# A hybrid layer on one core: the last pair's factors made one half later, the mixer called one step earlier, the first gates fetched later

## The chip, the cores and the metric

The kernel runs on one core of one Trainium2 chip. The time is device microseconds of one execution; before the change three runs gave 2416.04, 2421.66 and 2422.43 us, the median being 2421.66 us. One more execution was profiled, and every row below is from it.

## The reference

One layer (`DEPTH = 1`) on 512 tokens of 2048 features, all in float32:

```python
proj = rms_norm(x, g_mix) @ w_in                    # q, k, v, u, v_sgu, gate_a, gate_b
y_a = stick_breaking_attention(q, k, v) @ w_oa      # 8 heads of 128, output 1024 wide
s   = gelu(u) * (w_s @ layer_norm(gelu(v_sgu)) + b) # 8 groups, 128 x 128 mixing per 128 tokens
y_b = s @ w_ob
x = x + (sigmoid(gate_a) * y_a + sigmoid(gate_b) * y_b) @ w_out
x = x + square(relu(rms_norm(x, g_ff) @ w_ff1)) @ w_ff2    # hidden width 8192
```

## The kernel before, in words

**Arithmetic.** A float32 product is made from two parts of each operand, `hi` (a copy rounded to fp32r, made by ScalarE) and `lo` (the rest, a subtraction on VectorE). The function `mm3` issues three matmuls for each product: hi by hi, hi by lo and lo by hi; they stand at L72, L73 and L74. A weight piece is loaded into `w_raw` by SyncE's DMA queue, cast to `w_hi` by ScalarE and subtracted to `w_lo` by VectorE (L99 and L101 in `weight`, L113 and L114 in `split_to`). The pool of weight pieces has six buffers, three pairs of hi and lo.

**Order of the work.** Each engine runs its instructions strictly in the order that a planner at build time has chosen. The planner replays the program on its own costs and takes, for each engine, the earliest traced instruction that it thinks ready, so a later one can be taken ahead when it thinks the engine free and a buffer is there. The text of the kernel gives the tracing order. Beside the main loops there is a queue of tasks called `behind`: after each weight piece (or, in the last product, after each of seven sub-products) the loop calls `step()`, which takes one entry off that queue. `at_steps(steps)` puts a table of tasks, numbered by step, into the queue. `let(f)` traces a tiny GpSimd instruction (L814) that reads the newest `w_lo`, and orders the DMA issues in `f` behind it on GpSimd's queue.

**The product stage** (about 795 to 987 us). `by_column` first makes `ya` = attention output by `w_oa` in four column blocks j of 512, four weight pieces each, so 16 steps numbered 0 to 15; then `yb` = gated mixer output by `w_ob`, steps 16 to 31. Block j of `ya` ends with `evac_a`: four VectorE multiplications by the gate (`merged_a`, L836), which also free the accumulators in PSUM; the pool has five, and a block uses four. The attention output comes back from device memory as 16 tiles `oT` (two for each of 8 heads) through GpSimd's DMA queue, line L508 in `fetched`; 12 of them go into the pool `long`, whose buffers come free as the last input projection ends. On the same queue are fetched the gates (`gates(which, j)`, four tiles of 256 KB for one block) and the mixer's inputs (`fetch_mix(half)`, eleven tiles: `wsp`, `bs`, `vn` and `u`).

The mixer is called by half (four groups each). `split_mix` normalises `vn` (L788) and splits it. `mixed(g)` does for one group: matmuls (L801, L803), four VectorE instructions (L806, L808), a GpSimd multiplication (L810) and the split into `sT` (ScalarE's cast L113, VectorE's subtraction L114). `step()` for the last piece of a block is traced ahead of that block's `evac_a`.

**The last product** (`w_ff2`, about 1798 us to the end). Eight chunks f of 1024 hidden features; each has two halves g of the output columns, and each half seven sub-products with the names y11, y21, m7, m6, y22, m4, m5: 14 steps for one chunk. `strassen_tokens` works on two groups i of weights; `Sums.parts` makes the sums of weights that the names need (L186, L190, L192, L194 on VectorE) and splits them. `evac_y` adds the sub-products into `total` (L1041, L1044). The factors of the hidden activations were stored in device memory, and `fetch` brings them back on GpSimd's queue (L1001). For the last two pairs of hidden features, 30 and 31, the seven factors are made while the last product already runs, by `keeping` (L251 in `factor`, L113 and L114 in `halves`, the store at L967 on SyncE's queue): pair 31, the last, in chunk 0 and pair 30 in chunk 1. They are read only in chunk 7.

Of the kernel before, what the change touches and what calls it, by code (L numbers as in the profile page):

```python
# [35 lines left out]
def tile_hybrid_layer(ctx: ExitStack, tc: tile.TileContext, x, g_mix, w_in, g_q, g_k, ln_g, ln_b,  # L36
# [17 lines left out]
    def slot(name, dt=F32, pool=slots):  # L54
        return pool.tile([P, 512], dt, name=name, tag="slot")
# [4 lines left out]
    def aux(name):  # L60
        return ps_aux.tile([P, 512], F32, name=name, tag="aux")

    def tiny(n, name):
        return small.tile([P, n], F32, name=name, tag=f"tiny{n}")

    def f32(ap):
        return ap.bitcast(F32)
# [8 lines left out]
    state = {"load": None, "raw": raws}  # L76
    behind = collections.deque()
# [27 lines left out]
    def split(src, name, scale=None, pool=slots):  # L105

        hi, lo = slot(name + "_hi", F32R, pool), slot(name + "_lo", F32R, pool)
        split_to(hi, lo, src, scale)
        return hi, lo
# [396 lines left out]
    def fetched(src, name, dt=F32, pool=slots):  # L506
        t = slot(name, dt, pool)
        nc.gpsimd.dma_start(out=f32(t) if dt is F32R else t, in_=src)  # L508
        return t
# [171 lines left out]
    def at_steps(steps):  # L681
        behind.extend([lambda fs=steps.get(i, []): [f() for f in fs] for i in range(max(steps) + 1)])

    VC = 2 * SBW
    for half in range(2):
# [4 lines left out]
        if half:  # L690
            steps = collections.defaultdict(list)
# [63 lines left out]
    for i, item in enumerate(order):  # L755
# [6 lines left out]
        else:  # L762
            c0, n, func = item
# [7 lines left out]
    def gates(which, j):  # L771
        n = SGW // P + which * (D // P) + j * 4
        return [fetched(held_g[n + c], "gate") for c in range(4)]
# [4 lines left out]
    def fetch_mix(half):  # L778
        wsT.extend(fetched(held_s[half * 2 + i], "wsp", F32R) for i in range(2))
        bs[half] = fetched(held_s[4 + half], "bs")  # L780
        for tb in range(NTB):
            vn[tb, half] = fetched(held_v[half, tb], "vn")
        u.extend(fetched(held_g[half * 4 + g], "u") for g in range(4))

    def split_mix(half, blocks):
        for tb in blocks:
            t = vn[tb, half]
            nc.vector.tensor_scalar(out=t, in0=t, scalar1=mv[:, tb, 0:1], scalar2=rv[:, tb:tb + 1],  # L788
                                    op0=ALU.subtract, op1=ALU.mult)
            vn[tb, half] = split(t, "vn")  # L790

    def mixed(g):
        half, c = g // 4, (g % 4) * P
        both = wsT[g // 2][:, (g % 2) * 2 * P:(g % 2 + 1) * 2 * P]
        t = slot("smix")
        for pair in range(2):

            o = aux("mix").rearrange("p (b h i) -> p b h i", b=2, h=2)
            for b in range(2):
                vh, vl = (p[:, c:c + P] for p in vn[pair * 2 + b, half])  # L800
                nc.tensor.matmul(o[:, b].rearrange("p h i -> p (h i)"), lhsT=vh, rhs=both, start=True,  # L801
                                 stop=False)
                nc.tensor.matmul(o[:, b, 1], lhsT=vl, rhs=both[:, :P], start=False, stop=True)  # L803
            t3 = t[:, pair * 2 * P:(pair + 1) * 2 * P].rearrange("p (b i) -> p b i", b=2)
            gain = gT2[:, 32 + g:33 + g]
            nc.vector.scalar_tensor_tensor(out=t3, in0=o[:, :, 1, :], scalar=gain, in1=bs[half][:, c:c + P]  # L806
                                           .unsqueeze(1).to_broadcast([P, 2, P]), op0=ALU.mult, op1=ALU.add)
            nc.vector.scalar_tensor_tensor(out=t3, in0=o[:, :, 0, :], scalar=gain, in1=t3, op0=ALU.mult,  # L808
                                           op1=ALU.add)
        nc.gpsimd.tensor_tensor(out=t, in0=t, in1=u[g], op=ALU.mult)  # L810
        sT.append(split(t, "sT"))

    def let(f):
        gate = nc.gpsimd.tensor_tensor(out=tiny(4, "gate"), in0=f32(state["piece"])[:, 0, :4], in1=mhalf,  # L814
                                       op=ALU.mult)
        with tc.issue_after(gate.ins):
            f()

    with tc.issue_after(state["sum"].ins):
        ahead = collections.deque([gates(0, 0)])  # L820
    steps = collections.defaultdict(list)
    for half in range(2):
        steps[1 + 5 * half].append(lambda half=half: let(lambda: fetch_mix(half)))
        for i in range(2):
            steps[4 + i + 5 * half].append(lambda half=half, i=i: split_mix(half, (2 * i, 2 * i + 1)))
    for g in range(GROUPS):
        steps[7 + g + g // 4].append(lambda g=g: mixed(g))
    for i, wj in enumerate([(0, 1), (0, 2), (0, 3), (1, 0), (1, 1), (1, 2), (1, 3)]):
        steps[4 * i].append(lambda wj=wj: let(lambda: ahead.append(gates(*wj))))
    at_steps(steps)  # L830

    merged_a = []
# [121 lines left out]
    def keeping(p, act):  # L954

        ys = {}

        def keep(name):
            if name == "y11":
                for a in act:  # L960
                    nc.scalar.activation(out=a, in_=a, func=AF.Square)
            if name in ("y11", "y21", "y22"):
                h = act[name[1] == "2"]
                ys[name, 0] = halves(h[:, :HS] if name[2] == "1" else h[:, HS:])
            else:
                factor(ys, act, 0, name)
            nc.sync.dma_start(out=store[p // GROUP][HELD.index(name), p % GROUP], in_=f32(ys[name, 0]))  # L967

        return [lambda name=name: keep(name) for name in ("y11", "y21", "y22", "m7", "m6", "m4", "m5")]
# [43 lines left out]
    kept_last = []  # L1013
# [15 lines left out]
    for f in range(chunks):  # L1029
        ahead = {}  # L1030
        if kept_last:
            for task in keeping(*kept_last.pop()):
                behind.extend([task, lambda: None])
        for g in range(2):
            def evac_y(name, t, o):
                for half, c, op in takes[name]:
                    key = 2 * half + t, 2 * g + c
                    part = share[op][:, 2 * half + t:2 * half + t + 1]
                    if key not in total:
                        total[key] = slot("total")  # L1040
                        nc.scalar.activation(out=total[key], in_=o, func=AF.Copy, scale=part)  # L1041
                    else:
                        a = total[key]
                        nc.vector.scalar_tensor_tensor(out=a, in0=o, scalar=part, in1=a, op0=ALU.mult,  # L1044
                                                       op1=ALU.add)
                if f == chunks - 1:
                    for half, c in done[g].get(name, []):
                        tb, j = 2 * half + t, 2 * g + c
                        nc.sync.dma_start(out=out[tb * P:(tb + 1) * P, j * W:(j + 1) * W], in_=total[tb, j])

            def between(name):


                i = NAMES.index(name)
                if f == 0:
                    half, c, _ = takes[name][0]
                    gate = nc.gpsimd.tensor_tensor(out=tiny(4, "gate"), in0=total[2 * half + 1, 2 * g + c][:, :4],
                                                   in1=mhalf, op=ALU.mult)
                    with tc.issue_after(gate.ins):
                        if g == 0 and i + 4 < len(NAMES):  # L1060
                            lhs[NAMES[i + 4]] = fetch(0, NAMES[i + 4])
                        if g == 1:
                            ahead[name] = fetch(1, name)
                    return
                if (f, g) in ((2, 1), (3, 0)):
                    for n in (i, len(NAMES)) if i == len(NAMES) - 1 else (i,):
                        tb, j = n % NTB, 2 * (1 - g) + n // NTB
                        nc.gpsimd.dma_start(out=total[tb, j], in_=kept[tb, j], accum_op=ALU.add)
                i += g * 5
                if f < chunks - 1 and i < (5 if g == 0 else 7):  # L1070
                    ahead[NAMES[i]] = fetch(f + 1, NAMES[i])

            strassen_tokens(w_ff2[0], f * GROUP * 2 * P, g * 2 * W, lhs, evac_y, between,
                            loaded=f > 0, after=None if f or g else state["evac"],
                            last=f == chunks - 1 and g == 1)
        lhs = ahead
# [25 lines left out]
```

## Time and profile before

| what | before |
|---|---|
| profiled execution, its own time | 2421.55 us |
| its span, first to last instruction | 2419.8 us |
| median of three other runs | 2421.66 us |
| TensorE (PE) busy | 2401.8 us, 99% of the span |
| VectorE (DVE) busy | 1880.9 us, 78% |
| ScalarE (ACT) busy | 1283.1 us, 53% |
| mean granted TensorE clock | 0.999 |

A timeline row gives the start, the duration, the engine, the line of the kernel, the operation, output and inputs, and the count where several are merged; in brackets stand the idle time of the engine before it and what ended it. PE is TensorE's matmuls, POOL is GpSimd, SP is SyncE, whose instructions here are DMA issues ("SPq"). A wait row gives the total in us, how many there were and the longest. A row of a table of windows gives the stretch, its length, and for each engine busy time and count, then the granted clock (1.00 is full), the share of the DMA engines' time in use and GB/s.

### The profile page before, as it was taken

The page shows a single profiled execution, that of the slowest core. Times are in us where ns is not written, and L with a number is a line of the kernel's source. Part 1 is how long each engine was busy: PE and PEld are TensorE (multiplying, and loading weights), DVE is VectorE, ACT ScalarE, POOL GpSimd, SP SyncE. Part 2 cuts the span into 40 slices and gives each one's busy share as a digit, 9 for nine tenths or more (in the row PEclk, how much of TensorE's full clock was granted, in tenths as well). Part 3 has the DMA queues.
Part 4 walks back from the last instruction along what each step waited for, and adds up shares of the span by engine and source line. Part 5 has one row for each costly group of instructions (what it writes and reads, how often), then busy time and mean ns, then how long its engine had stood idle before and what let it go on. Part 6 is the DMA issues. An engine that isn't in the chain of part 4 may idle for free.

```text
span 2419.8 us, 34381 instructions
## 1 busy us (share of the span) xinstructions
PE 2401.8 (99%) x12452; PEld 2058.7 (85%) x12452; DVE 1880.9 (78%) x2555; ACT 1283.1 (53%) x1977; POOL 470.2 (19%) x584
## 2 busy tenths in 40 slices
PE   9999999999999999999999999999999999999999
PEld 8888888888888888888988888888877888888887
DVE  5566888777878465445788888888988998989987
ACT  5335666666666323233577777777765443333333
POOL 0101222222223322100000000001014334322210
PEclk9999999999999999999999999999999999999999
DMA  5557887878888933444488988888887999867753
GB/s 183 196 160 163 170 178 171 190 167 183 172 184 192 339 131 131 136 143 131 104 230 226 243 225 226 233 229 223 224 280 248 310 280 321 255 217 209 235 182 97
DMA packets 511769, 490.94 MB, mean 203 GB/s; under 512 B 20656, under 2 KB 401648, under 8 KB 511600
## 3 DMA queue, kind: packets, MB, share of 16 engines
q1 hardware_dynamic: 385232, 336.68, 43.7%
q0 software_dynamic: 126080, 151.55, 29.8%
q8 instruction: 98, 1.61, 0.3%
q10 hardware_dynamic: 288, 0.52, 0.1%
q14 instruction: 71, 0.58, 0.1%
HBM read 397.97 MB, written 89.65 MB: 202 GB/s over the span
## 4 chain that ended last, share of the span: by engine, by line
PE 59%; DMA 1%; DVE 1%; issue 0%; ACT 0%; DVEq 0%
PE q L223 9%; PE q L73 8%; PE q L74 8%; PE q L72 8%; PE fork L223 7%; PE q L226 5%; PE fork L226 3%; PE xo L72 2%; PE xo L74 2%; PE xo L73 2%; DMA w_raw<-in_w_ff_dram 1%; PE yb L72 1%; PE yb L73 1%; PE yb L74 1%; DVE w_lo L114 0%
## 5 line engine op out<-in xcount | busy, mean ns | idle before, releaser
L113 ACT CAST w_hi<-w_raw 128x1024 fp32r<-128x1024 f32 (+1 forms) x639 | 671.6, 1051 | 730.2 <-PE q L73 331.3
L114 DVE TENSOR_TENSOR w_lo<-w_raw,w_hi 128x1024 fp32r<-128x1024 f32 (+1 forms) x639 | 778.6, 1219 | 183.2 <-ACT w_hi L113 167.3
L223 PE MATMUL q<-ys,w_hi 128*128 128x512 f32 x1664 | 419.0, 393 | 2.3 <-ACT fork L231 2.3
L73 PE MATMUL q<-w_lo,ys 128*128 128x512 f32 x896 | 349.8, 390 | 5.1 <-DVE w_lo L114 5.1
L74 PE MATMUL q<-w_hi,ys 128*128 128x512 f32 x896 | 349.3, 390 | 0.0
L223 PEld LDWEIGHTS q<-ys,w_hi 128*128 128x128 f32 x1664 | 299.4, 189 | 56.8 <-ACT fork L231 2.8
L72 PE MATMUL q<-w_hi,ys 128*128 128x512 f32 x896 | 312.9, 390 | 0.2 <-DVE total L1044 0.2
L188 POOL DMA_DIRECT2D w_raw<-in_w_ff_dram x58 | 80.9, 1395 | 890.8 <-ACT act L993 214.3
L223 PE MATMUL fork<-ys,w_hi 128*128 128x512 f32 x968 | 242.2, 392 | 0.0
L226 PEld LDWEIGHTS q<-ys,w_lo 128*128 128x128 f32 x1664 | 225.2, 190 | 14.3
L226 PE MATMUL q<-ys,w_lo 128*128 128x256 f32 x1664 | 232.2, 282 | 0.0
L101 DVE TENSOR_TENSOR w_lo<-w_raw,w_hi 128x1024 fp32r<-128x1024 f32 x99 | 124.6, 1259 | 138.0 <-ACT w_hi L99 137.4
L99 ACT CAST w_hi<-w_raw 128x1024 fp32r<-128x1024 f32 x99 | 104.1, 1051 | 230.8 <-issue 83.3
L73 PEld LDWEIGHTS q<-w_lo,ys 128*128 128x128 f32 x896 | 168.6, 188 | 41.7 <-DVE w_lo L114 6.8
L223 PEld LDWEIGHTS fork<-ys,w_hi 128*128 128x128 f32 x968 | 175.9, 189 | 32.6
L72 PEld LDWEIGHTS q<-w_hi,ys 128*128 128x128 f32 x896 | 168.5, 188 | 35.7 <-issue 0.6
L74 PEld LDWEIGHTS q<-w_hi,ys 128*128 128x128 f32 x896 | 168.6, 188 | 35.0
L1001 POOL DMA_DIRECT2D ys<-store x224 | 127.3, 607 | 183.3 <-PE q L74 118.4
L226 PEld LDWEIGHTS fork<-ys,w_lo 128*128 128x128 f32 x968 | 132.0, 190 | 9.4
L1044 DVE SCALAR_TENSOR_TENSOR total<-q,plus,total 128x512 f32<-128x512 f32 x180 | 132.1, 745 | 4.6 <-PE q L74 4.6
L186 DVE TENSOR_TENSOR w_raw<-w_raw 128x1024 f32<-128x1024 f32 x91 | 111.2, 1223 | 30.8 <-DVE act L285 11.9
L226 PE MATMUL fork<-ys,w_lo 128*128 128x256 f32 x968 | 135.0, 282 | 0.0
(262 smaller groups left out, 3882.2 us busy)
## 6 DMA issues: line engine op xcount, KB each, us to landing
w_raw<-in_w_ff_dram SPq DMA_DIRECT2D x256, 512.0 KB, 5.2
w_raw<-in_w_in_dram SPq DMA_DIRECT2D x143, 512.0 KB, 5.3
ys<-store POOLq DMA_DIRECT2D x224, 256.0 KB, 6.6
w_raw<-in_w_ff_dram POOLq DMA_DIRECT2D x58, 512.0 KB, 6.8
w_raw<-in_w_in_dram POOLq DMA_DIRECT2D x56, 512.0 KB, 6.5
store<-ys_hi SPq DMA_DIRECT2D x90, 256.0 KB, 5.1
store<-ys_lo SPq DMA_DIRECT2D x90, 256.0 KB, 5.1
w_raw<-in_w_out_dram SPq DMA_DIRECT2D x32, 512.0 KB, 4.1
```

Source lines behind the costliest of these rows:

```text
L72: nc.tensor.matmul(o, lhsT=lh[0], rhs=rh[0], start=start, stop=False, **kw)
L73: nc.tensor.matmul(o, lhsT=lh[0], rhs=rh[1], start=False, stop=False, **kw)
L74: nc.tensor.matmul(o, lhsT=lh[1], rhs=rh[0], start=False, stop=stop, **kw)
L99: nc.scalar.copy(out=hi, in_=raw)
L101: nc.vector.tensor_tensor(out=lo, in0=raw, in1=f32(hi), op=ALU.subtract)
L113: nc.scalar.copy(out=hi, in_=src)
L114: state["lo"] = nc.vector.tensor_tensor(out=lo, in0=src, in1=f32(hi), op=ALU.subtract)
L186: nc.vector.tensor_tensor(out=self.a, in0=self.w11, in1=self.w21, op=ALU.add)
L223: nc.tensor.matmul(o, lhsT=hi[:, k, :], rhs=rhs[name][k], start=name in ("y11", "m7") and k == 0, stop=False, skip_group_check=True)
L226: nc.tensor.matmul(o[:, :HS], lhsT=lo[:, k, :], rhs=rhs[name][k][:, :HS], start=False, stop=k == KH - 1, skip_group_check=True)
L1001: nc.gpsimd.dma_start(out=f32(t), in_=store[f][HELD.index(name), p])
L1044: nc.vector.scalar_tensor_tensor(out=a, in0=o, scalar=part, in1=a, op0=ALU.mult, op1=ALU.add)
```

## The change

- **Gates of the first product.** `gates(0, 0)` was traced ahead of the product stage, on GpSimd's queue behind the tiles `oT`; it is now called at step 1, behind `fetch_mix(0)`. The other seven were called at steps 0, 4, 8, 12, 16, 20 and 24 and are now at 4, 7, 9, 12, 16, 20 and 24. The first one now has a `let` too, so there is one more tiny GpSimd instruction.
- **Mixer.** `split_mix` moves from steps 4, 5, 9 and 10 to 3, 4, 8 and 9; `mixed(g)` moves from steps 7, 8, 9, 10, 12, 13, 14, 15 to 6, 7, 8, 9, 11, 12, 13, 14. `fetch_mix` stays at steps 1 and 6.
- **Late pair.** In chunk 0 the seven tasks of `keeping` for pair 31 were traced after sub-products 0, 2, 4, ... 12; they now come after sub-products 7 to 13, one each, so all in the second half. Chunk 1 (pair 30) keeps the old spacing.

```diff
-    with tc.issue_after(state["sum"].ins):
-        ahead = collections.deque([gates(0, 0)])
+    ahead = collections.deque()
     steps = collections.defaultdict(list)
     for half in range(2):
         steps[1 + 5 * half].append(lambda half=half: let(lambda: fetch_mix(half)))
         for i in range(2):
-            steps[4 + i + 5 * half].append(lambda half=half, i=i: split_mix(half, (2 * i, 2 * i + 1)))
+            steps[3 + i + 5 * half].append(lambda half=half, i=i: split_mix(half, (2 * i, 2 * i + 1)))
     for g in range(GROUPS):
-        steps[7 + g + g // 4].append(lambda g=g: mixed(g))
-    for i, wj in enumerate([(0, 1), (0, 2), (0, 3), (1, 0), (1, 1), (1, 2), (1, 3)]):
-        steps[4 * i].append(lambda wj=wj: let(lambda: ahead.append(gates(*wj))))
+        steps[6 + g + g // 4].append(lambda g=g: mixed(g))
+    for i, n in enumerate((1, 4, 7, 9, 12, 16, 20, 24)):
+        steps[n].append(lambda i=i: let(lambda: ahead.append(gates(i // 4, i % 4))))
     at_steps(steps)
...
         if kept_last:
-            for task in keeping(*kept_last.pop()):
-                behind.extend([task, lambda: None])
+            late = keeping(*kept_last.pop())
+            for i, task in enumerate(late):
+                behind.extend([task, lambda: None] if f else [lambda: None] * (len(late) if i == 0 else 0) + [task])
```

## The prediction, as it was put on record

> **What bounds the kernel now.** I read the page first, then the waits of TensorE, then the timeline at each wait.
>
> ```profile
> span 2419.8 us, 34381 instructions
> ...
> PE 2401.8 (99%) x12452; PEld 2058.7 (85%) x12452; DVE 1880.9 (78%) x2555; ACT 1283.1 (53%) x1977; POOL 470.2 (19%) x584
> ```
>
> TensorE is busy for all but 18 us, and the change takes no matmul away, so it can only win what TensorE waits.
>
> ```profile
> PE q L73 <- DVE w_lo L114: 5.1, 3, 2.3
> PE ya L73 <- DMA oT<-held_o: 2.4, 1, 2.4
> ...
> PE yb L72 <- DVE merged_a L836: 2.0, 1, 2.0
> ...
> PE ya L72 <- DVE merged_a L836: 0.3, 1, 0.3
> ```
>
> These 9.8 us stand in the stages that the diff touches: 4.7 in the product stage (`ya`, `yb`), 5.1 in the last product (`q` at L73); what is left over of the 18 us lies elsewhere. The timeline of TensorE places the long ones:
>
> ```profile
> 820.43 0.50 PE L73 MATMUL ya<-oT,w_hi 128*128 128x512 f32 x1 [2.41 <-DMA oT<-held_o]
> ...
> 902.25 0.50 PE L72 MATMUL yb<-sT_hi,w_hi 128*128 128x512 f32 x1 [1.99 <-DVE merged_a L836]
> ...
> 1809.55 0.50 PE L73 MATMUL q<-w_lo,ys 128*128 128x512 f32 x1 [2.30 <-DVE w_lo L114]
> ...
> 1812.95 0.50 PE L73 MATMUL q<-w_lo,ys 128*128 128x512 f32 x1 [0.85 <-DVE w_lo L114]
> ...
> 1842.73 0.52 PE L73 MATMUL q<-w_lo,ys 128*128 128x512 f32 x1 [1.93 <-DVE w_lo L114]
> ```
>
> One wait has a second price. Windows of equal length, ahead of and behind two of these waits:
>
> ```profile
> 1805.54:1808.95 3.41, 1.71 (x8) 1.09 (x6) 3.41 (x4) 2.37 (x4) 2.19 (x5) 1.00 0.81 239
> 1808.95:1812.36 3.41, 2.56 (x10) 1.80 (x10) 3.41 (x4) 0.44 (x1) 0.42 (x1) 1.00 1.02 338
> 1839.67:1843.08 3.41, 1.48 (x8) 0.90 (x7) 3.41 (x6) 1.05 (x1) 2.59 (x1) 1.00 0.00 0
> 1843.08:1846.50 3.42, 3.42 (x10) 2.65 (x9) 3.42 (x6) 0.00 (x0) 1.46 (x1) 0.50 0.74 248
> ```
>
> Behind the wait that ended at 1842.73 the granted clock is 0.50 for 3.42 us: 1.7 us of work lost. The stretch ahead of it had 1.93 us of idle TensorE; the one ahead of 1808.95 had 1.70, and the clock stayed at 1.00. So between 1.70 and 1.93 idle us in such a stretch the clock halves here, and a wait cut into two stretches gets off free.
>
> **The change, part 1: the oT wait.** GpSimd's queue:
>
> ```profile
> 793.38 0.54 POOL L508 DMA_DIRECT2D gate<-held_g  x1 [0.23 <-DMA oT<-held_o]
> ...
> 803.21 0.55 POOL L508 DMA_DIRECT2D wsp<-held_s  x1 [0.34 <-DMA gate<-held_g]
> ...
> 811.92 0.54 POOL L508 DMA_DIRECT2D u<-held_g  x1 [0.86 <-issue]
> 812.72 0.54 POOL L508 DMA_DIRECT2D oT<-held_o  x1 [0.26 <-issue]
> ```
>
> The last three oT tiles stand behind 17 fetches: eight gates, then nine of the mixer's eleven. Each issue waits for an earlier landing, so the queue moves at (812.72 - 793.38) / 17 = 1.14 us a fetch. Now at most 15 can be ahead (eleven mixer fetches and four gates; the next four gates need step 4's weight piece), so the oT tiles come at least 2 x 1.14 = 2.3 us earlier. Bounds: 0, if the planner puts them further back, to -2.4, if they come ahead of the mixer. I take **-2.3**. The gates moved back are wanted when block 0 ends, which is after the matmul at 820.43, or 818.1 with the 2.3 taken off. As 15th fetch the last of them is issued at about 793.4 + 14 x 1.14 = 809.3 and, with the 7.7 us that the oT tile took (812.72 to 820.43), lands at 817.0: in time, by 1.1 us. The added tiny GpSimd instruction lies in queue time that waits for landings: nothing.
>
> **Part 2: the mixer.** VectorE and GpSimd:
>
> ```profile
> 849.67 0.69 DVE L114 TENSOR_TENSOR sT_lo<-smix,sT_hi 128x512 fp32r<-128x512 f32 x1 [2.06 <-ACT sT_hi L113]
> 850.28 2.48 DVE L836 TENSOR_TENSOR merged_a<-ya,gate 128x512 f32<-128x512 f32 x4
> ...
> 898.29 0.48 DVE L808 SCALAR_TENSOR_TENSOR smix<-mix,gT,smix 128x256 f32<-128x256 f32 x1
> 900.90 0.69 DVE L114 TENSOR_TENSOR sT_lo<-smix,sT_hi 128x512 fp32r<-128x512 f32 x1 [2.12 <-ACT sT_hi L113]
> 901.51 2.48 DVE L836 TENSOR_TENSOR merged_a<-ya,gate 128x512 f32<-128x512 f32 x4
> ```
>
> At 898.8 VectorE stands still for 2.1 us until GpSimd and ScalarE have finished group 7, with the evacuation of block 3 queued behind, and TensorE waits for its accumulator. Group 7 was at step 15, the last of block 3, and goes to 14; nothing of the mixer is left at 15. A step is 24 matmuls, 5.3 us (63 of them fill 14.00 us in a stretch shown below, 0.222 each), more than the 1.99: **-2.0**. In exchange, step 11, the last of block 2, gets group 4, the first of its half, as step 7 had group 0, with a wait of 0.3: **+0.3**. Bounds for both blocks: -0.3 to +2.0 each. The matmul and vector counts stay; the fetches of half 1 stay at step 6.
>
> **Part 3: the late pair.** VectorE in chunk 0, ahead of the wait at 1842.73:
>
> ```profile
> 1832.65 1.23 DVE L194 TENSOR_TENSOR w_raw<-w_raw 128x1024 f32<-128x1024 f32 x1 [2.88 <-DMA w_raw<-in_w_ff_dram]
> ...
> 1834.93 0.42 DVE L114 TENSOR_TENSOR ys<-act,ys 128x256 fp32r<-128x256 f32 x1
> 1835.27 1.22 DVE L190 TENSOR_TENSOR w_raw<-w_raw 128x1024 f32<-128x1024 f32 x1
> ...
> 1837.54 0.42 DVE L251 TENSOR_TENSOR act<-act 128x256 f32<-128x256 f32 x1
> 1837.87 1.22 DVE L194 TENSOR_TENSOR w_raw<-w_raw 128x1024 f32<-128x1024 f32 x1
> ...
> 1841.46 1.22 DVE L114 TENSOR_TENSOR w_lo<-w_raw,w_hi 128x1024 fp32r<-128x1024 f32 x1
> 1842.60 0.42 DVE L251 TENSOR_TENSOR act<-act 128x256 f32<-128x256 f32 x1
> ```
>
> From the landing that ended its wait at 1832.65, VectorE runs without a gap to the awaited w_lo. Two of the late pair's instructions stand between, 1835.27 - 1834.93 and 1837.87 - 1837.54: 0.67 us. SyncE's queue shows the stores:
>
> ```profile
> 1813.39 0.42 SPq L967 DMA_DIRECT2D store<-ys  x1
> ...
> 1821.98 0.91 SPq L967 DMA_DIRECT2D store<-ys  x1
> 1823.11 0.74 SPq L181 DMA_DIRECT2D w_raw<-in_w_ff_dram  x1
> 1835.38 0.34 SPq L967 DMA_DIRECT2D store<-ys  x1
> 1842.71 0.37 SPq L181 DMA_DIRECT2D w_raw<-in_w_ff_dram  x1
> ...
> 1819.00:1833.00 14.00, 14.00 (x63) 11.62 (x62) 9.26 (x10) 9.55 (x13) 5.47 (x12) 1.00 0.93 315
> ...
> 1866.00:1882.30 16.30, 16.30 (x73) 13.51 (x72) 14.61 (x16) 8.81 (x12) 11.15 (x16) 1.00 1.06 338
> ```
>
> The store at 1821.98 (256 KB) shares a stretch at 315 GB/s with the awaited load, up to 0.8 us; I take half, 0.4. Together **-1.1**, which leaves 0.8 of the wait, under the 1.70 that kept the clock: **-1.7**. Bounds: 0 to -3.6. The waits at 1809.55 and 1812.95 come ahead of the late pair's first store (1813.39); I leave them.
>
> What the second half takes on: three stores of 256 KB (1813.39, 1821.98, 1835.38), 0.79 MB or 2.3 us at 338 GB/s, where the DMA engines are already full (1.06), and VectorE, 14.61 of 16.30 us busy there, gets up to 0.84 us a step (L251 and ys). The cover is the weight pieces made ahead:
>
> ```profile
> 1864.16 1.23 DVE L114 TENSOR_TENSOR w_lo<-w_raw,w_hi 128x1024 fp32r<-128x1024 f32 x1 [1.19 <-ACT w_hi L113]
> ...
> 1868.50 0.62 PE L72 MATMUL q<-w_hi,ys 128*128 128x512 f32 x2
> ```
>
> With three pairs of buffers, the piece that is ready at 1865.4 is, as I count the pieces, the one used from 1868.5: 3.1 us of slack. I take **0**; without that cover the 2.3 us of transfers show: +2.3.
>
> Sum: -2.3 - 2.0 + 0.3 - 1.1 - 1.7 = -6.8, from the profiled execution's 2421.55 us (0.11 under the median; 1.75 of it lie outside the span): **2414.8 us**, own range 2412 to 2417.
>
> The Trainium skill (TensorE: Matmul & The Clock Gate, "What's actually happening") has the clock halve only after a whole idle window of about 3.4 us, a free-running one. The trace disagrees on the length, since 1.93 idle us sufficed; by the page the term -1.7 would be missing.
>
> **The rivals.**
> - *More goes*: with the late pair out, the planner may put y21's w_lo ahead of the weight sums that stand before it, and 2.30 + 0.85 vanish: 2411.6. For it: an instruction fewer in that stretch can turn the planner's choice. Against: none of those removed stands ahead of it.
> - *The half clock is met elsewhere*: work from 820 on comes some 4 us earlier, and the 2.30 us wait, now cut into 1.70 and the rest, may lie whole in one stretch: +1.7, 2416.5. For it: 4.0 is one stretch of 3.41 and 0.6, which on the grid of this execution would put the cut at the wait's end. Against: in other executions the waits at 820.43 and 902.25, both over 1.93, may have paid it too, and these go; so I don't add it to the sum. By the rule of the Trainium skill cited above, 1.93 us weren't the cause and the half clock stays, which comes to the same 2416.5.
> - *The late pair isn't out of the way*: the planner takes work ahead of its step (the L251 at 1842.60, after sub-product 7, can only be that of m5, traced after 12, as m6 and m4 wait for ys). Parts 1 and 2 alone: 2417.6.
> - *The product stage gives it back*: gates (0,2) are now called at step 7, ahead of block 1's evacuation. Four issues take 2.17 us (4 x 0.54); if VectorE's order waits for them, the 0.3 us wait grows by that and halves the clock: +3.9, 2418.7.
> - *Slower*: SyncE's queue is in order. Between 1823.85 and 1835.38 it stood 11.5 us at a store whose factor wasn't made, with nothing urgent behind. Now the stores stand among chunk 1's loads, whose sums VectorE's order has ahead of w_lo pieces. It decides from a delay above the 3.1 us slack: one such stand costs 11.5 - 3.1 + 1.7 = 10.1 (2424.9), two 20.2 (2435.0). Against: in that half VectorE keeps up.
>
> **How the numbers follow.** Chances: forecast 0.35, more 0.15, half clock elsewhere 0.15, late pair not out 0.10, given back 0.10, slower 0.15. About 0.3% (7.3 us) is what a measurement of this kernel can tell from no change: faster means under 2414.4, slower over 2428.9. Faster: not quite half of the forecast (0.16), all of "more" (0.15), and 0.04 of the half-clock case, since runs of one kernel differ by several us (2416.0 to 2422.4): 0.35. Slower: the part of the last case with two stands or more, 0.10. Same: 0.55. Range: down to 2409, all waits here gone with a us or two of spread, up to 2425, one stand of SyncE.
>
> **What would show it.** Part 1: the ya wait for oT under 0.5 us, the three oT issues before 811. Part 2: no wait for merged_a at yb; at most 0.3 at blocks 1 and 2. Part 3: no ys and L251 between 1832 and 1842, the wait there under 1 us, the clock 1.00 behind it; second half without waits. Wrong, if TensorE waits in the second half or SyncE stands over 3 us at a store there, or if new waits stand at blocks 1 and 2.

## The result, and the profile after

| kernel | median of its runs | range, runs | profiled execution | its span |
|---|---|---|---|---|
| before | 2419.73 us | 2416.03 to 2423.74, 22 | 2421.55 us | 2419.8 us |
| after | 2415.89 us | 2414.32 to 2418.44, 22 | 2416.23 us | 2414.2 us |

The ratio of after to before is 0.9984, with a 95% interval of 0.9977 to 0.9991: 3.8 us less. The two profiled executions are 5.6 us of span apart, since the one of before lies 1.8 us above its median of 22.

TensorE is as busy as before. Page of after, the engines:

```profile
PE 2401.7 (99%) x12452; PEld 2058.7 (85%) x12452; DVE 1881.9 (78%) x2555; ACT 1283.3 (53%) x1977; POOL 472.6 (20%) x585
```

So the whole difference is in what TensorE waits. Waits of TensorE in after, and its timeline at the long ones:

```profile
PE q L73 <- DVE w_lo L114: 3.3, 3, 1.9
PE ya L72 <- DVE merged_a L835: 1.7, 2, 1.3
PE q L223 <- ACT fork L231: 1.4, 2, 1.0
```

```profile
850.36 0.49 PE L72 MATMUL ya<-oT,w_hi 128*128 128x512 f32 x1 [1.34 <-DVE merged_a L835]
...
875.65 0.50 PE L72 MATMUL ya<-oT,w_hi 128*128 128x512 f32 x1 [0.38 <-DVE merged_a L835]
...
1804.75 0.50 PE L73 MATMUL q<-w_lo,ys 128*128 128x512 f32 x1 [1.90 <-DVE w_lo L114]
...
1905.18 0.50 PE L73 MATMUL q<-w_lo,ys 128*128 128x512 f32 x1 [0.68 <-DVE w_lo L114]
1908.87 0.50 PE L73 MATMUL q<-w_lo,ys 128*128 128x512 f32 x1 [0.68 <-DVE w_lo L114]
```

The waits for `oT` (2.41) and at `yb` (1.99) are gone, and so is the 1.93 before 1842.73. The wait at block 1 has grown from 0.31 to 1.34; block 2 has a new one of 0.38; chunk 1 of the last product, which had none, waits twice 0.68; and the pair 2.30 and 0.85 of 1809.55 and 1812.95 has become one wait of 1.90, with the half clock behind it. Windows of after on the grid of its clock records:

```profile
1802.29:1805.70 3.41, 1.51 (x7) 0.95 (x6) 3.41 (x4) 0.53 (x1) 2.29 (x5) 1.00 1.02 307
1805.70:1809.11 3.41, 3.41 (x10) 2.55 (x9) 3.41 (x4) 0.89 (x1) 0.00 (x0) 0.50 0.62 228
```

The balance: `oT` -2.4, `yb` -2.0, block 1 +1.0, block 2 +0.4, the wait for fork of the last sums (ScalarE) 1.36 to 0.45, -0.9, the waits of 1804 to 1813 -1.25 (3.15 to 1.90), the one at 1842 -1.9, chunk 1 +1.4, the half clock 1.7 both times: -5.7, against 5.6 between the spans.

### The profile page after: what moved, and what is told of

It reads as the page before. It is cut to its first block, busy times and chain, and to the rows that moved or that the text cites. A ratio compares the mean times of both kernels' runs of the same rounds, so it can differ in the third digit from the quotient of the medians.

```text
span 2414.2 us, 34394 instructions
## 1 busy us (share of the span) xinstructions
PE 2401.7 (99%) x12452; PEld 2058.7 (85%) x12452; DVE 1881.9 (78%) x2555; ACT 1283.3 (53%) x1977; POOL 472.6 (20%) x585
## 4 chain that ended last, share of the span: by engine, by line
PE 97%; DVE 1%; DMA 1%; ACT 1%; issue 0%; POOL 0%; SPq 0%; DVEq 0%; ACTq 0%; POOLq 0%
PE q L223 18%; PE fork L223 13%; PE q L226 9%; PE q L73 8%; PE q L74 8%; PE q L72 8%; PE fork L226 7%; PE xo L74 2%; PE xo L72 2%; PE xo L73 2%; PE v L72 1%; PE v L74 1%; PE v L73 1%; PE vg L72 1%; PE vg L73 1%; PE yb L73 1%
```

## The experiments

Theory: each of the three parts takes away the wait that it stands beside, as in the sum. Against it stand two others: that the late pair is not what makes VectorE late at 1842, and that the moves only hand the time to other waits. Each ratio is to the kernel before, run in the same session on the same chip, so small differences between ratios of different sessions are not to be read. None of these kernels leaves out any part of the computation.

| kernel | median, us | runs | ratio, 95% interval | profiled, us |
|---|---|---|---|---|
| gates_mixer | 2415.09 | 11 | 0.9979, 0.9970 to 0.9988 | 2414.59 |
| late_only | 2420.02 | 11 | 0.9998, 0.9989 to 1.0007 | 2419.72 |
| gates_only | 2416.20 | 11 | 0.9981, 0.9973 to 0.9990 | 2416.04 |
| mixer_only | 2417.48 | 11 | 0.9989, 0.9980 to 0.9998 | 2416.24 |
| hold | 2413.41 | 8 | 0.9974, 0.9964 to 0.9984 | 2411.97 |
| evac_first | 2412.00 | 6 | 0.9970, 0.9958 to 0.9981 | 2413.28 |
| late23 | 2414.42 | 11 | 0.9978, 0.9969 to 0.9987 | 2414.42 |
| joined | 2412.12 | 6 | 0.9968, 0.9956 to 0.9980 | 2413.16 |
| after_evac | 2412.55 | 6 | 0.9971, 0.9959 to 0.9983 | 2415.41 |
| joined_dma | 2410.96 | 5 | 0.9963, 0.9950 to 0.9975 | 2410.96 |
| joined_dma23 | 2407.78 | 5 | 0.9952, 0.9940 to 0.9965 | 2406.86 |

The kernel before had 2420.9 us in the session of the first four, 2420.11 in that of hold, evac_first, late23 and joined, and 2419.34 in the last.

### The parts by themselves

**gates_mixer**: the change without its last part.

```diff
-            late = keeping(*kept_last.pop())
-            for i, task in enumerate(late):
-                behind.extend([task, lambda: None] if f else [lambda: None] * (len(late) if i == 0 else 0) + [task])
+            for task in keeping(*kept_last.pop()):
+                behind.extend([task, lambda: None])
```

> Parts 1 and 2 alone (the late pair as before). Theory of separate terms: the waits at 820 (2.41) and 902 (1.99) are gone, the waits for merged_a at blocks 1 and 2 are 1.3 and 0.4 as in the changed kernel, chunk 0 keeps a wait near 1840 of about 1.9 with or without a half clock, chunk 1 has no wait: 2.5 to 3.5 us faster than before. Rival, that the late pair's part wins nothing on balance: this kernel is as fast as the whole change, 3.8 us faster.

**late_only**: the reverse, the last part alone, with gates and mixer as before.

> Part 3 alone. Theory of separate terms: the wait near 1842 (1.93 and its half clock) is gone, and chunk 1 waits about 1.4 us for w_lo near 1907 to 1917, where its loads land late: 0.5 to 1.5 us faster than before. Rival, that the waits in chunk 1 belong to the earlier start of the stage and not to the moved factors: no wait in chunk 1, 3 us faster.

**gates_only** and **mixer_only**: the first part alone, and the second alone.

```diff
 gates_only
-    with tc.issue_after(state["sum"].ins):
-        ahead = collections.deque([gates(0, 0)])
+    ahead = collections.deque()
...
+    for i, n in enumerate((1, 4, 7, 9, 12, 16, 20, 24)):
+        steps[n].append(lambda i=i: let(lambda: ahead.append(gates(i // 4, i % 4))))
...
 mixer_only
-            steps[4 + i + 5 * half].append(lambda half=half, i=i: split_mix(half, (2 * i, 2 * i + 1)))
+            steps[3 + i + 5 * half].append(lambda half=half, i=i: split_mix(half, (2 * i, 2 * i + 1)))
...
-        steps[7 + g + g // 4].append(lambda g=g: mixed(g))
+        steps[6 + g + g // 4].append(lambda g=g: mixed(g))
```

> Only the gates' fetches moved, mixer and late pair as before. If the place of the gates alone frees the queue: no wait for oT, the wait of 2.0 at yb stays. If gates (0,2) at step 7 hold up the evacuation of block 1: its wait grows from 0.3 to about 1.3 here. 1 to 2.5 us faster than before. Rival, that the oT wait needs the mixer's move too: wait of 2.4 stays, no gain.

> Only the mixer one step earlier, gates and late pair as before. Theory: no wait at yb (2.0 gone), the oT wait of 2.4 stays. If the mixer's own groups, 1 ahead of block 1's evacuation and 4 ahead of block 2's, make the new waits: 1.3 and 0.4 there, 0.5 to 1 us faster. Rival, that gates (0,2) make them: 0.3 or less at both, 2 us faster.

Measured: without the late pair's move the time is that of the whole change (0.9979 and 0.9984 of before, in two sessions); with it alone there is no change that can be told. The traces say where. The waits of TensorE in late_only:

```profile
PE q L73 <- DVE w_lo L114: 3.4, 5, 1.2
PE ya L73 <- DMA oT<-held_o: 3.1, 1, 3.1
```

And its timeline in the stretch where before had waited 1.93:

```profile
1834.54 0.50 PE L73 MATMUL q<-w_lo,ys 128*128 128x512 f32 x1 [0.55 <-DVE w_lo L114]
1846.43 0.50 PE L73 MATMUL q<-w_lo,ys 128*128 128x512 f32 x1 [0.20 <-DVE w_lo L114]
```

So the 1.93 has shrunk to 0.55 and 0.20; `oT`, which this edit does not touch, happens to take 3.1 here, and chunk 1 of the same trace waits 0.70 at 1912.84. But it is not certain that the late pair made the 1.93: in gates_mixer, which leaves the pair in its old place, the timeline has no more than this at that point:

```profile
1836.50 0.50 PE L73 MATMUL q<-w_lo,ys 128*128 128x512 f32 x1 [1.05 <-DVE w_lo L114]
```

Waits of gates_only, where the one for `oT` is missing:

```profile
PE q L73 <- DVE w_lo L114: 3.7, 3, 2.2
PE yb L72 <- DVE merged_a L835: 2.0, 1, 2.0
```

Waits of mixer_only, where the one at `yb` is missing:

```profile
PE ya L72 <- DVE merged_a L836: 1.7, 2, 1.3
PE ya L73 <- DMA oT<-held_o: 1.5, 1, 1.5
```

The gates' move takes away the wait for `oT` and leaves block 1 at 0.31; the mixer's move takes away the one at `yb` and brings 1.7 at blocks 1 and 2. By the medians the two alone are worth 4.7 and 3.4 us and together 5.8: no sum, since other waits shift with each (mixer_only has a new one of 0.5 for `vn_lo`). All three gains are larger than expected (1 to 2.5, 0.5 to 1, and 2.5 to 3.5 or 3.8): the waits for `w_lo` and `fork`, 5.1 and 2.3 us in the trace of before, come to 3.7 and 1.0 in gates_only, 3.7 and 1.4 in mixer_only, 3.9 and 1.4 in gates_mixer, though neither edit touches them. The waits for `w_lo` in the last product stay at 3.3 to 3.9 us in all of these traces and in that of after, wherever the late pair stands.

### Why blocks 1 and 2 wait: evac_first

**evac_first**: the gates' part alone; the evacuation of a block is traced ahead of `step()` of its last piece.

```diff
+            if kt + ck >= nk:
+                for c in range(w // P):
+                    evac(c, o[c])
             for _ in range(ck // CK):
                 step()
-        for c in range(w // P):
-            evac(c, o[c])
```

> The gates' fetches alone, and in the column product the evacuation of a block is put in ahead of the step that hangs on the block's last piece; mixer and late pair as before. Nothing is left out. If the waits for merged_a (1.99 at block 3 and 0.31 at block 1 with the gates alone) come from the mixer's last group standing ahead of merged_a in VectorE's order, both vanish, and the time is about 2 us below the gates alone (2416.2): near 2414. If the accumulator is late for another reason, the 1.99 stays and the time is 2416. If the evacuation put first delays the factors of the next block, a wait for sT_hi or sT_lo of 0.5 to 2 us takes its place: 2415 to 2418.

Measured: 2412.00 us, and no wait for `merged_a` is left. Waits of TensorE in evac_first, the longest group (the three others are 1.2, 1.0 and 0.2, for ones, fork and total):

```profile
PE q L73 <- DVE w_lo L114: 3.8, 4, 1.8
```

So those waits came from the order on VectorE, where the group of the block's last step stood ahead of `merged_a`. One edit of a few lines takes away what the mixer's move was to take away, without the price at blocks 1 and 2. **after_evac** is the same with the late pair's move of the change added:

> The gates' fetches and the late pair's move as in the change, the evacuation ahead of the last step in place of the mixer's move. Nothing is left out. Against the kernel with the same gates and evacuation but the late pair as before (2412.0): if the late pair's move is worth what the forecast gave it (2.8), near 2409; if it gives back in the second half of chunk 0 and in chunk 1 what it wins near 1840, 2411.5 to 2413, with waits of 0.5 to 1 each at 1900 to 1915 in the trace.

Measured: 2412.55 us, the same as evac_first, as far as two sessions can tell. Its seven waits for `w_lo` come to 5.1 us; 0.71 and 0.57 of them stand in chunk 1, at 1904.76 and 1908.35, as in after. Three more, 1.00, 0.17 and 0.26, stand at 1829.26, 1832.67 and 1841.16, where the late pair is no longer; evac_first, which has the pair there, waits 1.40 at 1834.64.

### Why the last product waits: hold, late23, joined

**hold**: gates and mixer as in the change, late pair as before; in chunk 0 the weight sums traced after y21 are ordered on VectorE behind y21's last `w_lo`.

```diff
-        banks = {}
+        banks, held = {}, None
...
-                    with tc.issue_after(after.ins) if after and name == "m7" else nullcontext():
+                    behind_of = held if held and not loaded else after if after and name == "m7" else None
+                    with tc.issue_after(behind_of.ins) if behind_of else nullcontext():
                         factors.append(ws[i].parts(name))
+                    if name == "y21" and i == 1:
+                        held = state["lo"]
```

> The gates' and the mixer's moves, the late pair as before, and in chunk 0 the weight sums (L186, L190, L194) that follow the last piece of y21 may be issued on VectorE only behind that piece's w_lo. Nothing is left out of the computation. If the waits near 1805 and 1808 (1.83 and 0.85 us with these two moves) come from VectorE's order, two L186 standing ahead of y21's w_lo, both fall below 0.5 and the time is 2 to 2.5 us below the kernel with the two moves (2415.1): near 2413. If they come from late data (the transfers or ScalarE's w_hi), the first wait stays over 1.5 and the time stays at 2415. If the sums so held back are then wanted themselves, the loss shows as new waits at 1811 to 1840 and the time is 2415 to 2417.

VectorE's timeline in gates_mixer; the awaited `w_lo` is the last row:

```profile
1798.73 2.36 DVE L186 TENSOR_TENSOR w_raw<-w_raw 128x1024 f32<-128x1024 f32 x2 [2.51 <-DMA w_raw<-in_w_ff_dram]
...
1803.28 1.22 DVE L114 TENSOR_TENSOR w_lo<-w_raw,w_hi 128x1024 fp32r<-128x1024 f32 x1
```

The same in hold, where it is the first:

```profile
1797.18 1.23 DVE L114 TENSOR_TENSOR w_lo<-w_raw,w_hi 128x1024 fp32r<-128x1024 f32 x1 [1.64 <-ACT w_hi L113]
1798.32 2.35 DVE L186 TENSOR_TENSOR w_raw<-w_raw 128x1024 f32<-128x1024 f32 x2
```

The awaited `w_lo` is made 6.1 us earlier, and of the waits of gates_mixer at 1804.55, 1807.95 and 1836.50 (1.83, 0.84 and 1.05) none is left. The data were there; VectorE's order was the cause of the first two. The one near 1836 is gone too, although the late pair stands where it stood before. But a new wait comes ahead of it, 1.30 us at 1822.17 for factors that GpSimd fetches, and by itself this could have covered the later one; joined_dma, below, has no wait there and decides it. GpSimd's timeline in hold, where the fetches are issued from 1816.29 on:

```profile
1810.36 5.98 POOL L1059 TENSOR_TENSOR gate<-total,mhalf 128x4 f32<-128x4 f32 x1 [7.53 <-DVE total L1046]
```

VectorE in the same stretch of hold, where the three `w_lo` of the last row are followed by a wait:

```profile
1811.33 2.35 DVE L192 TENSOR_TENSOR w_raw<-w_raw 128x1024 f32<-128x1024 f32 x2
...
1813.94 3.67 DVE L114 TENSOR_TENSOR w_lo<-w_raw,w_hi 128x1024 fp32r<-128x1024 f32 x3
```

The multiplication of four elements that orders the fetches spans 6 us. It ends at 1816.34, just when VectorE, gapless until then, pauses for the first time (0.10 us ahead of the third `w_lo`). The same instruction takes 0.21 us a little later.

**late23**: gates and mixer as in the change, and the two late pairs kept in chunks 2 and 3.

```diff
-        if kept_last:
+        if kept_last and f > 1:
```

> The gates' and the mixer's moves, and the two late pairs (factors and stores) kept in chunks 2 and 3 in place of 0 and 1. Nothing is left out. If the late pair's work is what makes the wait near 1836 to 1842 (1.06 with the two moves) and the ones near 1905 to 1914 (0.21, and 2.3 with the pair in the second half), both fall below 0.3 and the time is 1 us below the kernel with the two moves: near 2414, with waits in chunks 2 and 3 only if these have no room. If the wait near 1836 comes from the weight loads of the chunk's start alone, it stays at about 1 and the time is 2415. If chunks 2 and 3 have as little room as chunk 1, 1 to 2.5 us of waits appear there: 2415 to 2417.

Timeline of TensorE in late23, behind the waits at 1804.47 and 1807.88 (1.77 and 0.80, as in gates_mixer); it has no further one until 2386:

```profile
1830.67 0.50 PE L73 MATMUL q<-w_lo,ys 128*128 128x512 f32 x1 [0.74 <-DVE w_lo L114]
1834.08 0.50 PE L73 MATMUL q<-w_lo,ys 128*128 128x512 f32 x1 [0.16 <-DVE w_lo L114]
1842.57 0.50 PE L73 MATMUL q<-w_lo,ys 128*128 128x512 f32 x1 [0.20 <-DVE w_lo L114]
```

With no late pair in chunk 0 at all, 1.10 us is still lost from 1830 to 1843, as much as the 1.05 of gates_mixer. The waits of chunk 1, on the other hand, are gone. So the first case of the expectation failed in the one half and held in the other: the pair isn't needed for a wait near 1842, and it is needed for those of chunk 1. How much the pair added to the 1.93 of before isn't shown.

**joined**: evac_first and hold together, late pair as before.

> The gates' fetches, the evacuation ahead of the last step (in place of the mixer's move) and the weight sums held behind y21's w_lo; late pair as before. Nothing is left out. If both edits do what their single runs are to show, the waits for oT, for merged_a and near 1805 are gone: 2416.2 - 2.0 - 2.2, near 2412, below the kernel with the change (2415.9). If the held sums only move the wait, 2414. If neither works, 2416.

Measured: 2412.12 us, the time of the first of the three cases, but by the mechanism of the second: the held sums moved the wait. GpSimd's multiplication here spans 1808.57 to 1814.56, the factors behind it land late, TensorE waits 2.09 us at 1821.16 and pays the half clock.

### The multiplication on GpSimd, and room for the late pairs

**joined_dma**: joined, with a DMA of 16 bytes in place of the multiplication that orders the fetches in chunk 0. **joined_dma23**: that, with the edit of late23.

```diff
-                    gate = nc.gpsimd.tensor_tensor(out=tiny(4, "gate"), in0=total[2 * half + 1, 2 * g + c][:, :4],
-                                                   in1=mhalf, op=ALU.mult)
+                    gate = nc.gpsimd.dma_start(out=tiny(4, "gate")[:1], in_=total[2 * half + 1, 2 * g + c][:1, :4])
```

> The gates' fetches, the evacuation ahead of the last step, the weight sums held behind y21's w_lo, and in chunk 0 the four-element multiplication on GpSimd that orders the fetches of factors (line 1060 of the joined kernel) is replaced by a DMA of 16 bytes issued by GpSimd. Nothing is left out. In the joined kernel that multiplication spanned 1808.57 to 1814.56 and ended 0.06 us after VectorE's last gapless instruction (1814.50); the fetches behind it landed at 1821.02, and TensorE waited 2.09 us for them and had the half clock. If GpSimd's arithmetic waits for VectorE to stand still, a DMA does not: the fetches are issued 2 to 5 us earlier, the wait near 1821 and its half clock (3.9 us together) vanish, near 2408.5. If the fetches are late because of the awaited sum itself, the DMA's issue stands as long and the wait stays: 2412. If the fetches, now earlier, crowd out the weight loads, the wait goes to a w_lo at 1820 to 1840 of 1 to 2 us: 2410 to 2412.

> As the kernel before it in this list, with the two late pairs' factors and stores kept in chunks 2 and 3. Nothing is left out. If the late pairs cost chunks 0 and 1 anything and chunks 2 and 3 nothing (as the run with these moved alone had no wait from 1843 to the end, against 0.21 to 2.3 us), this is 0.5 to 1.5 us below that kernel; if the waits there have other causes, equal to it within 0.5.

GpSimd's timeline in joined_dma:

```profile
1810.47 0.52 POOL L1060 DMA_DIRECT2D gate<-total  x1 [9.53 <-DVE total L1047]
1810.98 2.15 POOL L1004 DMA_DIRECT2D ys<-store  x4
```

The fetches are issued at 1810.98 instead of 1814.50, while VectorE is as gapless as in joined, and the wait near 1821 is gone. The time is 2410.96: less is won than the 3.9 expected. Four short waits for `w_lo`, 1.9 us together, stand at 1806.65 (0.28), 1869.96 (0.43), 1903.81 and 1909.80 (0.92 and 0.25, in chunk 1), where joined had one of 0.67; and the trace has one of 1.16 at the start of the kernel, for `hT`, which no edit touches. Between 1806.65 and 1869.96 TensorE has no gap over 0.1 us, with the late pair in chunk 0 and no wait for fetches: so it was the order at the start of the chunk that the wait near 1836 came from, and hold had not merely covered it. With the late pairs in chunks 2 and 3 the four waits go too: 3.2 us less in the same session, twice the most that was expected. Only 1.9 of it are these waits; how much of the rest belongs to the wait at the start, which isn't in the trace of joined_dma23, isn't shown. In joined_dma23 TensorE has no gap over 122 us of the last product; its row of windows:

```profile
1798.00:1920.00 122.00, 122.00 (x539) 100.88 (x538) 106.79 (x107) 56.45 (x60) 47.14 (x84) 1.00 0.82 275
```

Its longest waits, 1.2 us for `ones` and 1.0 for `fork`, both ahead of the product stage, are in the kernel before as well.

At 2407.78 us, 0.9952 of before, it is the fastest of these kernels; its interval (0.9940 to 0.9965) ends below that of the change (0.9977 to 0.9991).

## Why the prediction was right, and where its steps were not

The time came out 1.1 us above the forecast, inside its own range and 0.16% under before, which is the case "within 0.3%". Part of that closeness is luck. The forecast starts from the profiled 2421.55 us, 1.8 above the median of 22, and takes off 6.8, where the medians differ by 3.8: two errors that go opposite ways. Between the two profiled executions the sum of -6.8 stands against a balance of -5.7; the terms under it agree less well than that.

**Part 1, the oT wait (-2.3): right.** GpSimd's queue in after:

```profile
807.14 0.56 POOL L508 DMA_DIRECT2D gate<-held_g  x1 [0.42 <-DMA vn<-held_v]
807.99 0.54 POOL L508 DMA_DIRECT2D gate<-held_g  x1 [0.29 <-DMA vn<-held_v]
809.30 0.54 POOL L508 DMA_DIRECT2D oT<-held_o  x1 [0.77 <-DMA vn<-held_v]
...
811.28 0.54 POOL L508 DMA_DIRECT2D oT<-held_o  x1 [0.37 <-issue]
```

The planner took the tiles ahead of the last two gates: 13 fetches stand before them, not 15. The third issue, at 811.28, misses the mark of 811 that was named, but the wait is zero, and so is the one that late gates would have made. gates_only gives the same on its own.

**Part 2, the mixer (-2.0 and +0.3): the size was off.** The wait at `yb` is gone, and block 2 pays 0.38, as said. The step that failed is that block 1 was left at its 0.3: step 7 lost group 0, as the working says, but it took in group 1, which the working doesn't price. VectorE in after:

```profile
843.56 1.22 DVE L101 TENSOR_TENSOR w_lo<-w_raw,w_hi 128x1024 fp32r<-128x1024 f32 x1 [1.53 <-PE mix L803]
844.70 0.68 DVE L114 TENSOR_TENSOR sT_lo<-smix,sT_hi 128x512 fp32r<-128x512 f32 x1
845.30 0.87 DVE L806 SCALAR_TENSOR_TENSOR smix<-mix,gT,bs 128x256 f32<-128x256 f32 x2
...
849.01 0.69 DVE L114 TENSOR_TENSOR sT_lo<-smix,sT_hi 128x512 fp32r<-128x512 f32 x1 [2.05 <-ACT sT_hi L113]
849.62 0.69 DVE L835 TENSOR_TENSOR merged_a<-ya,gate 128x512 f32<-128x512 f32 x1
```

The `sT_lo` at 844.70 belongs to group 0; it and the weight piece stand ahead of group 1, whose own chain ends with the 2.05 us for ScalarE and the `merged_a` behind it. That the order makes these waits, evac_first shows; that group 0's `sT_lo` makes the 1.34 longer than the 0.38 of block 2, is argued from these rows. The part was worth -0.6 in the trace of after, not -1.7. The rival *the product stage gives it back* named this place, but another cause: the fetches of gates (0,2) at step 7 are in gates_only too, and block 1 waits 0.31 there.

**Part 3, the late pair (-1.1 and -1.7): the mechanism was wrong in the main.** Two instructions of the pair stood in VectorE's row ahead of the awaited `w_lo`, and a store shared the load's time; both were read rightly and didn't decide. late23 has no late pair there and waits 1.10, gates_mixer has it and waits 1.05; hold and joined_dma have it too and wait nothing. What was late is VectorE's order at the start of the chunk, 30 us before: the sums ahead of y21's `w_lo`. The rival *more goes* saw that order; it took another instruction to turn it than any that the change moves. That after shows no wait at 1842 is no proof for the pair either: its 1.90 and the 1.7 of the half clock, 3.6 us, are what gates_mixer and late23 lose in waits there (3.7 each). But gates_only and evac_first, with a half clock and the pair in place, lose 5.1 and 4.9; so what the pair adds behind a half clock stays open.

The half clock was met elsewhere, as the rival of that name has it: the 1.90 of 1804.75 lies whole in one stretch in after, where the 2.30 before had been cut. That rival's 2416.5 is 0.3 from the profiled 2416.23. It is not a fixed price of the change: in gates_mixer the 1.83 at the same place was cut by the grid (at most 1.07 us idle in one stretch), and the clock stayed full.

The second half, costed at 0: in the rest of chunk 0 there is no wait, and SyncE's stand before the store of 1861.60, some 4 us and so over the 3 us that were named as a sign of being wrong, held up nothing that TensorE waited for. Queue of SyncE in after:

```profile
1857.28 0.37 SPq L181 DMA_DIRECT2D w_raw<-in_w_ff_dram  x1
1861.60 4.48 SPq L966 DMA_DIRECT2D store<-ys  x2
```

But the bill comes in chunk 1, whose own late pair then follows without a pause. DMA issues of after in a stretch of chunk 1 (1884 to 1893) with three weight loads; the last number is the median from issue to landing:

```profile
w_raw<-in_w_ff_dram SPq DMA_DIRECT2D x3, 512.0 KB, 14.7
```

The same three in before (1892 to 1901.5):

```profile
w_raw<-in_w_ff_dram SPq DMA_DIRECT2D x3, 512.0 KB, 11.1
```

And in joined_dma23 (1881 to 1888), without a late pair there:

```profile
w_raw<-in_w_ff_dram SPq DMA_DIRECT2D x3, 512.0 KB, 9.6
```

VectorE's row of after for the second of these loads:

```profile
1902.76 1.23 DVE L186 TENSOR_TENSOR w_raw<-w_raw 128x1024 f32<-128x1024 f32 x1 [4.71 <-DMA w_raw<-in_w_ff_dram]
```

And of before:

```profile
1907.48 1.23 DVE L186 TENSOR_TENSOR w_raw<-w_raw 128x1024 f32<-128x1024 f32 x1 [1.29 <-DMA w_raw<-in_w_ff_dram]
```

From 1846 to that stretch after issues 8 stores of 256 KB, before 5; all three stretches move 387 to 405 GB/s with the DMA engines full. VectorE waits 4.71 instead of 1.29, and TensorE twice 0.68. Not all of the 1.4 is the move's: with the pair in its old place gates_mixer waits 0.21 in chunk 1, and its three loads from 1884 to 1893 take 12.0 us; late_only waits 0.70 against nothing in before, after_evac 1.28 against 0.61 in evac_first. So the move adds 0.7 to 1.2 us there. The term of 0 was too small; the bound of +2.3, for transfers that show, was above it. Part 3 as a whole is nothing: late_only 0.9998 (a gain of 2.8 us, 0.9988, lies just outside its interval), after_evac beside evac_first the same. Its idea, room for the late pair, was good and half a chunk too short: in chunks 2 and 3 the pairs cost nothing that can be seen.

**Why the sum still came out.** What was missed above (1.1 in the mixer, 1.7 of the half clock, 1.4 in chunk 1) was made good, all but 1.1 us, by what was not forecast: 0.8 more at 1842 than the 1.1, 1.25 at 1804 to 1813, and 0.9 at the last sum's fork, which ScalarE releases. That wait lies between less than 0.1 and 1.4 in these traces, whatever the edit; its cause stays open. So it is by luck that the parts add up. The times before 820 and after 1920 don't differ.

## What to carry to other kernels

Before work is moved away from a wait, look in the engine's own order for what stands ahead of the awaited instruction though it isn't needed yet, and where the data landed: here an ordering edit of a few lines took away 3.7 us of waits that moving other work had not, and 1.3 came back as a new wait until that was mended too. A task that hangs on the last piece of a block belongs behind the block's evacuation. And the transfers taken out of one stretch were paid here in the next one where the DMA engines are full, some tens of microseconds later: find the stretch with room first.

## What the runs showed of the hardware

**A half clock can follow 1.80 idle us in a stretch of 3.41.** The stretches lie on a grid that runs on through the whole execution: in the five traces with a half clock it begins 526 to 538 whole stretches of 3.413 us after the first entry of the clock's record. In thirteen traces the stretches of the product stage and of the last product with 1.76 us of idle TensorE or less kept the clock. Five with more, all with matmuls on both sides, halved it for the next 3.41 us: 1.80 (evac_first), 1.90 (after), 1.93 (before), 2.09 (joined), 2.21 (gates_only). The two nearest to each other stand in the windows of late23 and of evac_first, each with the stretch behind it (idle is the length less the busy time of PE, the next column). Late23:

```profile
1801.05:1804.46 3.41, 1.65 (x8) 1.03 (x6) 3.41 (x4) 1.61 (x2) 2.62 (x5) 1.00 0.99 305
1804.46:1807.87 3.41, 2.60 (x10) 1.80 (x10) 3.41 (x4) 0.99 (x1) 0.00 (x0) 1.00 0.82 302
```

Evac_first:

```profile
1799.05:1802.46 3.41, 1.61 (x8) 1.01 (x7) 3.41 (x4) 1.18 (x2) 2.61 (x5) 1.00 0.87 306
1802.46:1805.87 3.41, 3.41 (x10) 2.63 (x9) 3.41 (x5) 0.25 (x1) 0.00 (x0) 0.50 0.73 261
```

One stretch doesn't fit. In joined, the stretch in which the last matmul ends has 1.90 idle us too, and behind it the clock stays full to the end of the span:

```profile
2405.57:2408.98 3.41, 1.51 (x7) 0.93 (x5) 1.50 (x2) 0.00 (x0) 0.00 (x0) 1.00 0.27 104
2408.99:2411.10 2.11, 0.00 (x0) 0.00 (x0) 0.00 (x0) 0.00 (x0) 0.00 (x0) 1.00 0.21 77
```

So these traces give no sharp border of idle time; what else counts stays open. A wait of 3.10 (late_only, `oT`) went free, cut into 1.75 and 1.35. The Trainium skill (TensorE: Matmul & The Clock Gate, "What's actually happening") has a free-running window of 3413 ns, which these records bear out, and puts the throttled state after at least one idle window; here just over half a window idle sufficed five times.

**A tiny multiplication on GpSimd can take as long as a whole run of VectorE's instructions.** The multiplication of four elements took 0.21 us where VectorE stood still, and 5.98 and 5.99 us in hold and joined, where it ended 0.06 us after the end of VectorE's gapless run. In joined:

```profile
1808.57 5.99 POOL L1060 TENSOR_TENSOR gate<-total,mhalf 128x4 f32<-128x4 f32 x1 [7.53 <-DVE total L1047]
```

It doesn't always wait for a pause, though. In before it was through in 0.52 us, 0.06 us after the end of one VectorE instruction (1806.00 + 1.22), while VectorE ran on without a gap:

```profile
1806.76 0.52 POOL L1057 TENSOR_TENSOR gate<-total,mhalf 128x4 f32<-128x4 f32 x1 [15.74 <-ACT total L1041]
```

```profile
1806.00 1.22 DVE L190 TENSOR_TENSOR w_raw<-w_raw 128x1024 f32<-128x1024 f32 x1
1807.14 1.22 DVE L194 TENSOR_TENSOR w_raw<-w_raw 128x1024 f32<-128x1024 f32 x1
```

Why the next end of an instruction sufficed there, and only that of the run in hold and joined, stays open. The DMA issue in its place took 0.52 us under the load of joined. The Trainium skill (GPSIMD Engine Reference, "Key points") says that GpSimd shares its SBUF interfaces with VectorE and contends with VectorE's instructions that have two SBUF inputs; the runs agree, and they add a price: the rest of one such instruction in before, a run of six in hold and joined.
